# Half of the residual's transposes taken over by transposing transfers, at six of eight stage inputs

## The chip, the cores and the metric

The kernel runs on one core of a Trainium2 chip. A core has a matrix engine (TensorE, "PE" in the profile; its weight loads are "PEld"), three engines for elementwise work (VectorE "DVE", ScalarE "ACT", GpSimd "POOL"), and SyncE ("SP"), which here only issues DMA transfers. Matmuls write into PSUM banks; everything else lives in SBUF. The metric is the device time of one execution in microseconds (us); less is better.

## The reference

A decoder trunk of two layers on a stream `h` of 256 rows by 1024 columns, float32. Each layer has a half-step SwiGLU ffn, a token mixer (layer 0: a gated linear recurrence; layer 1: attention with a forget gate) and another ffn, each between two RMS norms. Layer 1's keys, values and gates come from the stream as it is after layer 0.

```python
for layer in range(DEPTH):
    if layer == N_A_LAYERS:
        k, v, c = shared_kv(h, kv_norm_g, w_kv, w_fgate, b_fgate)
    f = swiglu(rms_norm(h, ffn1_pre_g[layer]), ...)          # (silu(x @ w_gate) * (x @ w_up)) @ w_down
    h = h + 0.5 * rms_norm(f, ffn1_post_g[layer])
    hn = rms_norm(h, mix_pre_g[layer])
    m = recurrent_block(hn, ...) if layer < N_A_LAYERS else forgetting_attention(hn, ...)
    h = h + rms_norm(m, mix_post_g[layer])
    f = swiglu(rms_norm(h, ffn2_pre_g[layer]), ...)
    h = h + 0.5 * rms_norm(f, ffn2_post_g[layer])
```

What matters for the change is the step between two sub-layers: `h` is updated, and the next matmuls need `h`, scaled by a gain per column, with its columns on the partitions, that is, transposed.

## The kernel before

The 256 rows are two row tiles, t = 0 and t = 1, of 128 rows each. `h[t]` is 128 partitions by 1024 columns. A matmul contracts over partitions, so the input of a projection is kept as eight **k tiles**, each 128 columns of `h` transposed to 128 by 128.

All products are float32 made of two parts: each weight is split into `whi` (a rounded copy, ScalarE, L173) and `wlo` (the rest, VectorE, L177); each input into `xhi` (ScalarE, L235) and `xlo` (VectorE, L240). Three matmuls stand for one: hi by hi, hi by lo, lo by hi (L183 to L185, L428 to L432).

The weights come in units of up to 128 by 1024, loaded by SyncE into one of five raw buffers (`raw`) and split into one of nine pairs. One unit used for one row tile is a slot of six matmuls of 512 columns, some 1.36 us. `run()` interleaves the two row tiles: tile 0 is some slots ahead of tile 1, and each unit is used by both. `defer(n, fn)` calls `fn` n + 1 slots later, so the place at which something is issued hangs on the count of slots. TensorE's order is that of the code. On the other engines a scheduler chooses the order, with two means to steer it: `tc.high_priority()`, and `tc.keep_in_program_order`, which pins an instruction among the others so pinned.

**A stage's end** is `enter(t, dests, ...)` (L271). ScalarE sums squares of the accumulators (`junk`, L205), GpSimd makes `nv` and `rstd` (L198, L200), VectorE multiplies the accumulators by the gain (`t`, from PSUM, L284), and then updates `h` in two halves of 512 columns (L297). Some slots later (`defer(wait, inputs)`) comes `inputs()`: eight PE transposes (L226, `to_tp`, four for each half of the columns, into a PSUM bank each); per destination VectorE multiplies a bank by the next norm's gains (`xg`, L234), ScalarE makes `xhi` of it, VectorE `xlo`; and `stat(t)` starts the next norm's sums (ScalarE L205, GpSimd L198 and L200). There is one destination, save after layer 0, where there are two: layer 1's ffn (`xhi`, `xlo`) and the shared keys and values (`zhi`, `zlo`).

**The transposing transfer** is in the kernel already, for the ffn's products and for keys and queries: `planes` (GpSimd copies float32 into two planes of 16-bit halves; L210, L527), `swap` (SyncE issues a DMA that transposes 16-bit blocks of 128 by 128; L214, L535; pinned in SyncE's order), `join` (GpSimd copies the turned halves back into float32; L218, L540).

The eight stage inputs that `inputs()` serves, by the time of their transposes in the profile:

| | stage that ends | tile | transposes at, us | destinations |
|---|---|---|---|---|
| unchanged | mixer, layer 0 | 0 | 296.64 | 1 |
| place 1 | mixer, layer 0 | 1 | 304.52 | 1 |
| place 2 | second ffn, layer 0 | 0 | 475.42 | 2 |
| place 3 | second ffn, layer 0 | 1 | 485.84 | 2 |
| place 4 | first ffn, layer 1 | 0 | 703.31 | 1 |
| unchanged | first ffn, layer 1 | 1 | 713.72 | 1 |
| place 5 | mixer, layer 1 | 0 | 771.37 | 1 |
| place 6 | mixer, layer 1 | 1 | 783.14 | 1 |

Of the kernel before, what the change touches and what calls it, by code (L numbers as in the profile page):

```python
# [9 lines left out]
F32 = mybir.dt.float32  # L10
# [33 lines left out]
def trunk_kernel(ctx: ExitStack, tc: tile.TileContext, A: dict, out: bass.AP):  # L44
# [13 lines left out]
    def nm(s):  # L58
        uid[0] += 1
        return f"{s}_{uid[0]}"  # L60
# [168 lines left out]
    def x_upper(tp, dest, n):  # L229

        gi, xh, xl = dest
        xg = hpool.tile([P, 4, P], F32, tag="t1", name=nm("xg"), bufs=2)
        g = gT[:, gi + 4 * n:gi + 4 * n + 4].unsqueeze(2).to_broadcast([P, 4, P])
        nc.vector.tensor_tensor(xg, tp.rearrange("p (a b) -> p a b", a=4), g, ALU.mult)  # L234
        nc.scalar.activation(xh[:, 4 * n:4 * n + 4, :], xg, AF.Copy)  # L235
        return xg

    def x_lower(xg, dest, n):
        gi, xh, xl = dest
        nc.vector.tensor_tensor(xl[:, 4 * n:4 * n + 4, :], xg, xh[:, 4 * n:4 * n + 4, :].bitcast(F32), ALU.subtract)  # L240

    def to_x(tps, dest):

        with tc.high_priority():
            xg = [x_upper(tps[n], dest, n) for n in range(2)]
            for n in range(2):
                x_lower(xg[n], dest, n)

    def to_x_tiles(tps, dest):

# [15 lines left out]
    def stat(t):  # L266
        ss = new_ss()
        square_sum(h[t], ss[:, 0:1])
        rs[t] = rstd_of(ss, 1)

    def enter(t, dests, pf, gb, half, last=False, normed=False, wait=3):  # L271

        f = 1.0 / 16 if half else 1.0 / 32
        ss = new_ss()
        t1 = []
        urgent = tc.high_priority()
        urgent.__enter__()
        for n in range(2):
            square_sum(pf[n], ss[:, n:n + 1], f)
        for n in range(2):  # L280
            if n == 1 and last:
                r = rstd_of(ss, 2, f, nc.vector)
            t1.append(hpool.tile([P, 512], F32, tag="t1", name=nm("t1"), bufs=2))
            nc.vector.tensor_tensor(t1[n], pf[n], gb[:, n * 512:(n + 1) * 512], ALU.mult)  # L284
        if not last:
            r = rstd_of(ss, 2, f)

        sp, aq = nc.sync, nc.scalar
        pieces = [(n * 512, 512, None) for n in range(2)]
        if last:  # L290
            pieces = ([(0, 1024, sp)] if t == 0 else
                      [(0, 256, sp), (256, 256, aq), (512, 256, sp), (768, 256, aq)])
        for c, m, q in pieces:
            hn = h[t][:, c:c + m]
            for a in range(c, c + m, 512):
                n = min(m, 512)
                nc.vector.scalar_tensor_tensor(h[t][:, a:a + n], t1[a // 512][:, a % 512:a % 512 + n], r[:, 0:1],  # L297
                                               h[t][:, a:a + n], ALU.mult, ALU.add)
            if last:
                q.dma_start(out[0, t * P:(t + 1) * P, c:c + m], hn)  # L300
        urgent.__exit__(None, None, None)
        if last:
            return

        def inputs():
            tps = [to_tp(h[t], n) for n in range(2)]
            for dest in dests:
                to_x(tps, dest)
            stat(t)

        def norm():
            with tc.high_priority():
                normed_x()

        def normed_x():
            ss = new_ss()
            for n in range(2):
                square_sum(h[t][:, n * 512:(n + 1) * 512], ss[:, n:n + 1])
            rs[t] = rstd_of(ss, 2)
            hn = []  # L320
            for n in range(2):
                hn.append(hpool.tile([P, 512], F32, tag="t1", name=nm("hn"), bufs=2))
                nc.vector.tensor_scalar(hn[n], h[t][:, n * 512:(n + 1) * 512], rs[t][:, 0:1], None, ALU.mult)

            def go():
                tps = []
                for n in range(2):
                    tp = gtbank()
                    for j in range(4):
                        nc.tensor.transpose(tp[:, j * P:(j + 1) * P], hn[n][:, j * P:(j + 1) * P], ident)  # L330
                    tps.append(tp)
                to_x_tiles(tps, dests[0])
            defer(6, go)

        if normed:
            norm()
            settled[0] = True
        else:
            defer(wait, inputs)
# [152 lines left out]
    def ahead(i, fn):  # L492
# [5 lines left out]
            return prep()  # L498
        items[i] = (both, work)

    def ffn_items(pool_of, wg, wu, wd, post_g, next_dests, last=False, normed=False):
        hid = {}
        sil = {}
        box = {}

        def hid_tiles(t):
            if t not in hid:
                hid[t] = (pool_of().tile([P, 22, P], F32R, tag=f"hhi{t}", name=nm("hhi"), bufs=1),
                          pool_of().tile([P, 22, P], F32R, tag=f"hlo{t}", name=nm("hlo"), bufs=1))
            return hid[t]  # L510

        def post_gate(c0, nn):
            def f(t, ps):
                s = pool_of().tile([P, 512], F32, tag="sil", name=nm("sil"), bufs=2)
                nc.scalar.activation(s[:, :nn], ps, AF.Silu, scale=rs[t][:, 0:1])  # L515
                sil[t] = s
            return f

        def post_up(c0, nn):
            def f(t, ps):  # L520
                hh, hl = hid_tiles(t)
                s = sil[t][:, :nn]
                pr = pool_of().tile([P, 512], F32, tag="prod", name=nm("prod"), bufs=2)
                nc.vector.scalar_tensor_tensor(pr[:, :nn], ps, rs[t][:, 0:1], s, ALU.mult, ALU.mult)  # L524
                halves = hpool.tile([P, 512], F32, tag="t1", name=nm("pl"), bufs=2).bitcast(U16)[:, :2 * nn]
                turned = pr.bitcast(U16)[:, :2 * nn].rearrange("p (a b) -> p a b", b=P)
                nc.gpsimd.tensor_copy(halves.rearrange("p (h f) -> p h f", h=2),  # L527
                                      pr[:, :nn].bitcast(U16).rearrange("p (f h) -> p h f", h=2))
                defer(2, lambda: hidden_T(halves, turned, hh, hl))

            def hidden_T(halves, turned, hh, hl):

                m, k0 = nn // P, c0 // P
                keep = tc.keep_in_program_order
                keep(nc.sync.dma_start(turned, halves, transpose=True))  # L535
                hv = hh[:, k0:k0 + m, :].rearrange("p a b -> p (a b)")
                lv = hl[:, k0:k0 + m, :].rearrange("p a b -> p (a b)")

                def join():
                    nc.gpsimd.tensor_copy(halves.rearrange("p (f h) -> p h f", h=2),  # L540
                                          turned.rearrange("p (h a) b -> p h (a b)", h=2))

                def parts():
                    x = halves.bitcast(F32)
                    keep(nc.scalar.activation(hv, x, AF.Copy))  # L545
                    keep(nc.vector.tensor_tensor(lv, x, hv.bitcast(F32), ALU.subtract))  # L546
                defer(3, join)
                defer(7, parts)
            return f

        i0 = len(items)
        for i in range(5):
            proj_items(wg, i * 512, 512, main_x, post_gate(i * 512, 512))
            proj_items(wu, i * 512, 512, main_x, post_up(i * 512, 512))

        last_up = post_up(2560, 256)

        def post_both(t, pg, pu):
            post_gate(2560, 256)(t, pg)
            last_up(t, pu)  # L560

        pair_items(wg, wu, 2560, 256, main_x, post_both)

        def load_gb():
            box["gb"] = gain_bcast(post_g)

        ahead(i0 + 24, load_gb)

        def post_down(t, accs):
            enter(t, next_dests(t), accs, box["gb"], True, last, normed)  # L570

        row_items(wd, [P] * 22, lambda t, k: (hid[t][0][:, k, :], hid[t][1][:, k, :]), post_down, 4 if last else 2)
        return i0

# [644 lines left out]
    def post_q(n):  # L1219
        return lambda t, ps: heads_T(ps, t, n, HD ** -0.5, att["q"][t])  # L1220

    for n in range(2):
        proj_items(A["attn_w_q"][0], n * 512, 512, main_x, post_q(n))
    n_q[0] = len(items)
    row_items(A["attn_w_o"][0], [P] * 8, lambda t, k: (att["oh"][t][:, k, :], att["ol"][t][:, k, :]),
              lambda t, accs: enter(t, [main_dest(GI[("ffn2", 1)], t)], accs, gbox["mix1"], False, wait=4),
              rows0=1, late=True)
    ahead(n_q[0] + 2, load_gb("mix1", A["mix_post_g"][1]))
    n_att = len(items)
# [240 lines left out]
```

## Time and profile before

| | |
|---|---|
| median of three runs | 966.05 us (965.71 to 967.69) |
| the profiled execution | 965.92 us, its span 964.2 us |
| granted TensorE clock | 0.999 |
| TensorE busy | 955.9 us, 99% of the span |
| VectorE, ScalarE, GpSimd busy | 640.7, 527.6, 218.2 us |
| PE transposes of `h` (L226) | 64, in eight groups of 0.87 to 0.88 us |

A row of the timeline reads: start and length in us, engine, line, operation, output <- inputs, their shapes, how many alike follow one another (x2), and in brackets the idle time before it and what released it. Rows of the chain in order of time have a start, a length and what it was. Lines are those of the kernel before; in the kernel after they are higher by 14 from L270 on and by up to 35 further down.

### The profile page before, as it was taken

The numbers are of one execution on the slowest core, as the hardware profiler recorded it, in microseconds if no ns is written. First come the engines' busy times: TensorE is split into PE (matmuls) and PEld (weight loads), VectorE is DVE, ScalarE is ACT, GpSimd is POOL, SyncE is SP. The second block draws the span as 40 slices with busy tenths as digits, with TensorE's granted clock in tenths as the row PEclk, the third lists the DMA queues.
The fourth block names the chain that finished last, engine by engine and source line by source line (L and its number), as shares of the span: only waits on it lengthen the run. The fifth ranks groups of instructions, "written<-read, shape, count | busy, mean of one in ns | idle before, by whom it ended". The sixth has DMA issues, their size and how long they took to land.

```text
span 964.2 us, 12866 instructions
## 1 busy us (share of the span) xinstructions
PE 955.9 (99%) x4575; PEld 791.3 (82%) x4575; DVE 640.7 (66%) x845; ACT 527.6 (55%) x750; POOL 218.2 (23%) x221
## 2 busy tenths in 40 slices
PE   9999999999999999999999999999999999999997
PEld 6888888898878888888898888888887788888886
DVE  6658674678997666664686566665488876666642
ACT  7546453568886555443565455444366855444431
POOL 2712330130001323230003522234022012232200
PEclk9999999999999999999999999999999999999999
DMA  8787995475346787775558979878773468777731
GB/s 286 226 258 225 256 284 197 142 228 163 119 123 219 209 236 211 205 242 196 135 182 278 253 219 258 230 216 265 226 256 97 133 199 236 207 222 233 223 109 44
DMA packets 148934, 198.79 MB, mean 206 GB/s; under 512 B 67166, under 2 KB 85958, under 8 KB 148742
## 3 DMA queue, kind: packets, MB, share of 16 engines
q1 hardware_dynamic: 146182, 191.06, 65.6%
q0 software_dynamic: 2080, 6.38, 2.1%
q8 instruction: 36, 0.59, 0.2%
q10 hardware_dynamic: 608, 0.53, 0.2%
q14 instruction: 28, 0.23, 0.1%
HBM read 182.19 MB, written 3.16 MB: 192 GB/s over the span
## 4 chain that ended last, share of the span: by engine, by line
PE 95%; DVE 2%; ACT 1%; issue 1%; POOL 0%; DMA 0%; POOLq 0%; DVEq 0%; ACTq 0%
PE mm L428 16%; PE mm L429 16%; PE mm L432 16%; PE mm L183 13%; PE mm L185 13%; PE mm L184 13%; PE gt L795 2%; PE mm L1305 1%; PE mm L190 1%; PE mm L191 1%; PE mm L192 1%; PE gt L226 1%; ACT pe L1181 1%; DVE wlo L177 0%; PE tr L127 0%
## 5 line engine op out<-in xcount | busy, mean ns | idle before, releaser
L177 DVE TENSOR_TENSOR wlo<-raw,whi 128x1024 fp32r<-128x1024 f32 (+5 forms) x329 | 418.0, 1276 | 230.7 <-ACT whi L173 228.3
L173 ACT ACTIVATE whi<-raw 128x1024 fp32r<-128x1024 f32 (+5 forms) x329 | 341.9, 1045 | 308.6 <-PE mm L432 119.2
L428 PE MATMUL mm<-whi,xhi 128*128 128x512 f32 x656 | 256.6, 391 | 0.0
L429 PE MATMUL mm<-wlo,xhi 128*128 128x512 f32 x656 | 255.5, 389 | 0.0
L432 PE MATMUL mm<-whi,xlo 128*128 128x512 f32 x656 | 202.1, 389 | 0.0
L428 PEld LDWEIGHTS mm<-whi,xhi 128*128 128x128 f32 x656 | 123.2, 188 | 25.9 <-issue 0.7
L432 PEld LDWEIGHTS mm<-whi,xlo 128*128 128x128 f32 x656 | 123.1, 188 | 25.8 <-DVE xlo L240 0.2
L429 PEld LDWEIGHTS mm<-wlo,xhi 128*128 128x128 f32 x656 | 123.2, 188 | 25.4 <-DVE wlo L177 0.3
L183 PE MATMUL mm<-whi,hhi 128*128 128x512 f32 x352 | 137.2, 390 | 0.0
L185 PE MATMUL mm<-whi,hlo 128*128 128x512 f32 x352 | 137.0, 389 | 0.0
L184 PE MATMUL mm<-wlo,hhi 128*128 128x512 f32 x352 | 136.9, 389 | 0.0
L540 POOL COPY pl<-prod 128x1024 uint16<-128x1024 uint16 (+1 forms) x48 | 69.9, 1456 | 174.4 <-DMA prod<-pl 174.4
L527 POOL COPY pl<-prod 128x1024 uint16<-128x1024 uint16 (+1 forms) x48 | 66.3, 1382 | 151.9 <-DVE prod L524 86.8
L183 PEld LDWEIGHTS mm<-whi,hhi 128*128 128x128 f32 x352 | 66.1, 188 | 13.7
L185 PEld LDWEIGHTS mm<-whi,hlo 128*128 128x128 f32 x352 | 66.1, 188 | 13.7
L184 PEld LDWEIGHTS mm<-wlo,hhi 128*128 128x128 f32 x352 | 66.1, 188 | 13.6
L198 POOL TENSOR_SCALAR nv<-ss 128x1 f32<-128x1 f32 x22 | 9.6, 437 | 268.7 <-ACT junk L205 268.7
L524 DVE SCALAR_TENSOR_TENSOR prod<-mm,rstd,sil 128x512 f32<-128x512 f32 (+1 forms) x48 | 33.8, 703 | 29.5 <-PE mm L432 25.9
L515 ACT ACTIVATE sil<-mm,rstd 128x512 f32<-128x512 f32 (+1 forms) x48 | 31.0, 649 | 32.9 <-PE mm L432 25.0
L546 DVE TENSOR_TENSOR hlo<-pl,hhi 128x512 fp32r<-128x512 f32 (+1 forms) x48 | 41.2, 858 | 3.7 <-ACT hhi L545 3.7
L183 PE MATMUL mm<-whi,xhi 128*128 128x512 f32 (+1 forms) x112 | 42.8, 382 | 0.0
L185 PE MATMUL mm<-whi,xlo 128*128 128x512 f32 (+1 forms) x112 | 42.5, 379 | 0.0
(223 smaller groups left out, 1054.6 us busy)
## 6 DMA issues: line engine op xcount, KB each, us to landing
raw<-in_ffn_w_down_dram SPq DMA_DIRECT2D x88, 512.0 KB
raw<-in_ffn_w_up_dram SPq DMA_DIRECT2D x80, 512.0 KB
raw<-in_ffn_w_gate_dram SPq DMA_DIRECT2D x78, 512.0 KB
raw<-in_rg_w_in_dram SPq DMA_DIRECT2D x10, 504.0 KB
raw<-in_rg_w_out_dram SPq DMA_DIRECT2D x10, 504.0 KB
raw<-in_ffn_w_gate_dram SPq DMA_DIRECT2D x19, 256.0 KB
raw<-in_ffn_w_up_dram SPq DMA_DIRECT2D x16, 256.0 KB
raw<-in_rg_w_in_dram SPq DMA_DIRECT2D x8, 512.0 KB
```

The lines of the kernel that those rows point to most:

```text
L173: up = nc.scalar.activation(hi[:parts, c:c + m], rawv[:, c:c + m], AF.Copy)
L177: nc.vector.tensor_tensor(lo[:parts, c:c + m], rawv[:, c:c + m], hi[:parts, c:c + m].bitcast(F32), ALU.subtract)
L183: nc.tensor.matmul(ps, xh, wh, start=first, stop=False)
L184: nc.tensor.matmul(ps, xh, wl, start=False, stop=False)
L185: nc.tensor.matmul(ps, xl, wh, start=False, stop=last)
L428: nc.tensor.matmul(ps, get_x(t, k)[0], u.hi[:, c], start=k == 0, stop=False)
L429: nc.tensor.matmul(ps, get_x(t, k)[0], u.lo[:, c], start=False, stop=False)
L432: nc.tensor.matmul(ps, get_x(t, k)[1], u.hi[:, c], start=False, stop=k == nk - 1)
L524: nc.vector.scalar_tensor_tensor(pr[:, :nn], ps, rs[t][:, 0:1], s, ALU.mult, ALU.mult)
L527: nc.gpsimd.tensor_copy(halves.rearrange("p (h f) -> p h f", h=2), pr[:, :nn].bitcast(U16).rearrange("p (f h) -> p h f", h=2))
L540: nc.gpsimd.tensor_copy(halves.rearrange("p (f h) -> p h f", h=2), turned.rearrange("p (h a) b -> p h (a b)", h=2))
L546: keep(nc.vector.tensor_tensor(lv, x, hv.bitcast(F32), ALU.subtract))
```

## The change

At places 1 to 6 the columns 512 to 1023 of `h` (k tiles 4 to 7) no longer go through PE transposes. Right after `h` is updated, GpSimd copies them into planes. `inputs()` makes four transposes in place of eight, and after `stat(t)` SyncE issues the transposing transfer; one slot later GpSimd is given the joining copy, and two (tile 0) or four (tile 1) slots later the joined tile is scaled on VectorE per destination (from SBUF; `turned_to_x`), copied into `xhi` on ScalarE and subtracted into `xlo` on VectorE. The scale and the copy are pinned in their engines' order. The buffers: for tile 0 old buffers of the ffn's products, or of the queries; for tile 1 the buffers named "t1" and "junk". Two stage inputs stay as they were.

```diff
     def to_x(tps, dest):
         with tc.high_priority():
-            xg = [x_upper(tps[n], dest, n) for n in range(2)]
-            for n in range(2):
-                x_lower(xg[n], dest, n)
+            xg = [x_upper(tp, dest, n) for n, tp in enumerate(tps)]
+            for n, v in enumerate(xg):
+                x_lower(v, dest, n)
+
+    def turned_to_x(v, dests, more):
+        with tc.high_priority():
+            xs = []
+            for i, (gi, xh, xl) in enumerate(dests):
+                xg = v if i == len(dests) - 1 else more()
+                g = gT[:, gi + 4:gi + 8].unsqueeze(2).to_broadcast([P, 4, P])
+                xs.append(xg.rearrange("p (a b) -> p a b", a=4))
+                tc.keep_in_program_order(
+                    nc.vector.tensor_tensor(xs[i], v.rearrange("p (a b) -> p a b", a=4), g, ALU.mult))
+                tc.keep_in_program_order(nc.scalar.activation(xh[:, 4:, :], xs[i], AF.Copy))
+            for xg, dest in zip(xs, dests):
+                x_lower(xg, dest, 1)
...
-    def enter(t, dests, pf, gb, half, last=False, normed=False, wait=3):
+    def enter(t, dests, pf, gb, half, last=False, normed=False, wait=3, spare=None):
...
+        by_transfer = not normed and (spare or t == 1) and not (half and len(dests) == 1 and t == 1)
+        if by_transfer:
+            a = spare() if t == 0 else hpool.tile([P, 512], F32, tag="t1", name=nm("hp"), bufs=2)
+            with tc.high_priority():
+                planes(a.bitcast(U16), h[t][:, 512:])
+
         def inputs():
-            tps = [to_tp(h[t], n) for n in range(2)]
+            tps = [to_tp(h[t], n) for n in range(1 if by_transfer else 2)]
             for dest in dests:
                 to_x(tps, dest)
             stat(t)
+            if by_transfer:
+                b = spare() if t == 0 else spool.tile([P, 512], F32, tag="junk", name=nm("ht"), bufs=1)
+                with tc.high_priority():
+                    swap(b.bitcast(U16), a.bitcast(U16))
+                defer(0, lambda: join(a.bitcast(U16).rearrange("p (f h) -> p h f", h=2), b.bitcast(U16)))
+                defer(1 + 2 * t, lambda: turned_to_x(a, dests, spare))
...
+    def old_products():
+        return pools["f"].tile([P, 512], F32, tag="prod", name=nm("hp"), bufs=2)
...
-            enter(t, next_dests(t), accs, box["gb"], True, last, normed)
+            enter(t, next_dests(t), accs, box["gb"], True, last, normed, spare=old_products)
...
+    q_parts = [1, 0]
+
+    def old_q():
+        return att["q"][0].rearrange("p a b -> p (a b)").rearrange("p (s f) -> p s f", s=2)[:, q_parts.pop(), :]
...
-              lambda t, accs: enter(t, [main_dest(GI[("ffn2", 1)], t)], accs, gbox["mix1"], False, wait=4),
+              lambda t, accs: enter(t, [main_dest(GI[("ffn2", 1)], t)], accs, gbox["mix1"], False, wait=4,
+                                    spare=old_q),
```

**VectorE at place 2**, from the update of `h0` (tile 0) to that of `h1` (tile 1), before; a name's number only tells buffers apart, `gt` is a bank of transposes:

```order
L297 SCALAR_TENSOR_TENSOR h_74<-t_807_4254,rstd_4258,h_74 128x512
L177 TENSOR_TENSOR wlo_4271<-raw_4268,whi_4270 128x1024
L177 TENSOR_TENSOR wlo_4283<-raw_4280,whi_4282 128x1024
L234 TENSOR_TENSOR xg_4302<-gt_4292,gT 128x512
L234 TENSOR_TENSOR xg_4305<-gt_4297,gT 128x512
L177 TENSOR_TENSOR wlo_4329<-raw_4325,whi_4328 128x720
L240 TENSOR_TENSOR xlo<-xg_4302,xhi 128x4x128
L240 TENSOR_TENSOR xlo<-xg_4305,xhi 128x4x128
L234 TENSOR_TENSOR xg_4310<-gt_4292,gT 128x512
L234 TENSOR_TENSOR xg_4313<-gt_4297,gT 128x512
L177 TENSOR_TENSOR wlo_4342<-raw_4338,whi_4341 128x720
L240 TENSOR_TENSOR zlo_4246<-xg_4310,zhi_4245 128x4x128
```

(Then a second zlo, the two `t` and the two halves of `h1`.) The same stretch after, from the first xg on; `hp` is the joined tile, and L258 its scale:

```order
L234 TENSOR_TENSOR xg_4298<-gt_4293,gT 128x512
L234 TENSOR_TENSOR xg_4302<-gt_4293,gT 128x512
L177 TENSOR_TENSOR wlo_4319<-raw_4315,whi_4318 128x720
L240 TENSOR_TENSOR xlo<-xg_4298,xhi 128x4x128
L240 TENSOR_TENSOR zlo_4245<-xg_4302,zhi_4244 128x4x128
L177 TENSOR_TENSOR wlo_4333<-raw_4329,whi_4332 128x720
L258 TENSOR_TENSOR hp_4342<-hp_4261,gT 128x512
L298 TENSOR_TENSOR t_841_4380<-mm_3946,gb_3331 128x512
L258 TENSOR_TENSOR hp_4261<-hp_4261,gT 128x512
L240 TENSOR_TENSOR xlo<-hp_4342,xhi 128x4x128
L298 TENSOR_TENSOR t_842_4382<-mm_3947,gb_3331 128x512
L240 TENSOR_TENSOR zlo_4245<-hp_4261,zhi_4244 128x4x128
```

Two of four xg are gone, and two scales stand later, the first after the last wlo and the second between the two `t`; `h1` follows behind this row in both.

**VectorE at place 4**, from the two wlo behind `h0` to `h1`'s `t`, before:

```order
L177 TENSOR_TENSOR wlo_1211_6228<-raw_1209_6225,whi_1210_6227 128x1024
L177 TENSOR_TENSOR wlo_1214_6240<-raw_1212_6237,whi_1213_6239 128x1024
L234 TENSOR_TENSOR xg_1217_6259<-gt_1215_6249,gT_89 128x512
L234 TENSOR_TENSOR xg_1218_6262<-gt_1216_6254,gT_89 128x512
L177 TENSOR_TENSOR wlo_1225_6277<-raw_1223_6274,whi_1224_6276 128x1024
L240 TENSOR_TENSOR xlo_91<-xg_1217_6259,xhi_90 128x4x128
L240 TENSOR_TENSOR xlo_91<-xg_1218_6262,xhi_90 128x4x128
L177 TENSOR_TENSOR wlo_1228_6289<-raw_1226_6286,whi_1227_6288 128x1024
L177 TENSOR_TENSOR wlo_1231_6301<-raw_1229_6298,whi_1230_6300 128x1024
L284 TENSOR_TENSOR t1_1238_6327<-mm_1153_5890,gb_1024_5266 128x512
```

and after, from the xg on:

```order
L234 TENSOR_TENSOR xg_1217_6253<-gt_1216_6248,gT_89 128x512
L177 TENSOR_TENSOR wlo_1225_6269<-raw_1223_6266,whi_1224_6268 128x1024
L240 TENSOR_TENSOR xlo_91<-xg_1217_6253,xhi_90 128x4x128
L177 TENSOR_TENSOR wlo_1228_6282<-raw_1226_6279,whi_1227_6281 128x1024
L258 TENSOR_TENSOR hp_1209_6216<-hp_1209_6216,gT_89 128x512
L177 TENSOR_TENSOR wlo_1231_6297<-raw_1229_6294,whi_1230_6296 128x1024
L298 TENSOR_TENSOR t1_1238_6323<-mm_1153_5887,gb_1024_5263 128x512
L240 TENSOR_TENSOR xlo_91<-hp_1209_6216,xhi_90 128x4x128
L298 TENSOR_TENSOR t1_1239_6325<-mm_1154_5888,gb_1024_5263 128x512
L311 SCALAR_TENSOR_TENSOR h1_75<-t1_1238_6323,rstd_1241_6329,h1_75 128x512
```

Here the scale stands ahead of the last wlo, and its xlo between the two `t`.

**GpSimd at place 2**, from tile 0's `rstd` on, after; before, the three rows with `hp` or of its joining are not there, and the rest stands in the same order:

```order
L200 TENSOR_TENSOR rstd_809_4257<-nv_808_4255,mhalf_85 128x1
L212 COPY hp_810_4261<-h0_74 128x1024
L198 TENSOR_SCALAR nv_822_4309<-ss_820_4306 128x1
L200 TENSOR_TENSOR rstd_823_4311<-nv_822_4309,mhalf_85 128x1
L220 COPY hp_810_4261<-hp_824_4313 128x2x512
L198 TENSOR_SCALAR nv_843_4384<-ss_838_4375 128x1
L200 TENSOR_TENSOR rstd_844_4386<-nv_843_4384,mhalf_85 128x1
L212 COPY hp_845_4390<-h1_75 128x1024
```

The planes copy (L212) has come in behind tile 0's `rstd`, and the joining copy (L220) ahead of the `nv` and `rstd` from which tile 1's `h` is updated.

## The prediction

> **What bounds the kernel now.** I read the page's first part and its chain first, then the chain in order of time around the transposes, then VectorE's and TensorE's rows at each place.
>
> ```profile
> PE 955.9 (99%) x4575; PEld 791.3 (82%) x4575; DVE 640.7 (66%) x845; ACT 527.6 (55%) x750; POOL 218.2 (23%) x221
> PE 95%; DVE 2%; ACT 1%; issue 1%; POOL 0%; DMA 0%; POOLq 0%; DVEq 0%; ACTq 0%
> ```
>
> TensorE is busy for 955.9 of 964.2 us and carries 95% of the chain. So a microsecond taken from TensorE is a microsecond gained, as long as its inputs are there; and a microsecond for which it waits is lost whole, because nothing behind it has slack to give back. The other engines have room on average, but the average doesn't tell about the stage ends, where the change acts.
>
> **What is removed.** At each of the six places four of eight PE transposes go. The chain in order of time (start, length, what) has these groups, place 1 to place 6:
>
> ```profile
> 304.52 0.87 PE gt L226 x8
> 475.42 0.87 PE gt L226 x8
> 485.84 0.87 PE gt L226 x8
> 703.31 0.87 PE gt L226 x8
> 771.37 0.88 PE gt L226 x8
> 783.14 0.87 PE gt L226 x8
> ```
>
> Eight cost 0.87, so four cost 0.435, and six places give 6 x 0.435 = 2.61 us. All of it lies on the chain. That is the most that the change can bring: 965.92 - 2.61 = 963.3 against the profiled execution's own 965.92 us (0.13 below the median of the runs, which I neglect). VectorE keeps its count: where it multiplied a transposed bank (xg, read from PSUM), it now multiplies the joined tile (the scale, read from SBUF), once per destination.
>
> **What is added, alone.** Per place a copy into planes and a joining copy on GpSimd, and one transposing transfer on SyncE. The kernel has all three already, on the ffn's products. Rows of GpSimd, of SyncE's queue, of the chain and of the waits (total us, count, longest):
>
> ```profile
> 49.99 1.04 POOL L527 COPY pl<-prod 128x1024 uint16<-128x1024 uint16 x1 [3.13 <-DVE prod L524]
> 51.05 1.24 SPq L535 DMA_TRANSPOSE prod<-pl  x1
> 56.78 1.34 POOL L540 COPY pl<-prod 128x1024 uint16<-128x1024 uint16 x1 [5.76 <-DMA prod<-pl]
> 732.70 3.06 DMA htok<-pl
> POOL pl L540 <- DMA prod<-pl: 174.4, 46, 10.1
> ```
>
> Planes take 1.04, SyncE's issue 1.24, the joining copy 1.34. From issue to joined copy it is 3.1 in a quiet queue (the row at 732.70), 5.7 where other transfers stand in the way (51.05 to 56.78), 3.8 on the mean over 46 waits (174.4 / 46), 10.1 at the worst. At places 2 and 4 the transfer stands ahead of the next weight load in SyncE's order, and the loads before it were issued long ago or wait behind it, so I take 3.1 to 3.5 there. The weight loads behind it are held for the 1.24 us of the issue and for GpSimd's planes; five raw buffers stand between a load and its use, so I cost that at nothing. If that cover went, it would cost up to 1.24 a place.
>
> **What the copies do to VectorE.** A planes copy and a joining copy, each beside VectorE's work, then hlo alone, and a joining copy with a VectorE row that reads PSUM:
>
> ```profile
> 361.88 1.22 DVE L177 TENSOR_TENSOR wlo<-raw,whi 128x1024 fp32r<-128x1024 f32 x1
> 363.01 1.53 DVE L546 TENSOR_TENSOR hlo<-pl,hhi 128x512 fp32r<-128x512 f32 x1
> 362.09 1.90 POOL L527 COPY pl<-prod 128x1024 uint16<-128x1024 uint16 x1 [5.84 <-ACT hhi L545]
> ...
> 91.38 1.79 DVE L546 TENSOR_TENSOR hlo<-pl,hhi 128x512 fp32r<-128x512 f32 x1
> 90.44 2.25 POOL L540 COPY pl<-prod 128x1024 uint16<-128x1024 uint16 x1 [6.65 <-DMA prod<-pl]
> ...
> 64.80 0.68 DVE L546 TENSOR_TENSOR hlo<-pl,hhi 128x512 fp32r<-128x512 f32 x1
> 101.34 2.32 POOL L540 COPY pl<-prod 128x1024 uint16<-128x1024 uint16 x1 [3.21 <-DMA prod<-pl]
> 102.37 0.74 DVE L524 SCALAR_TENSOR_TENSOR prod<-mm,rstd,sil 128x512 f32<-128x512 f32 x1
> ```
>
> The planes copy at 362.09 begins during a wlo and takes 1.90 where it takes 1.04 alone: it stood for 0.86 until that wlo ended at 363.10. Then hlo took 1.53 where it takes 0.68 alone, 0.85 more. With the joining copy at 90.44 it is 2.25 for 1.34, and hlo 1.79, which is 1.11 more. So the two engines exclude each other here, and VectorE pays 0.85 per planes copy and 1.11 per joining copy. The row at 102.37 reads PSUM, lies inside the joining copy at 101.34, and takes 0.74; its group of 48 has a mean of 0.70 (x48, 703 ns on the page), so it is not delayed. Bounds of one pair: 0 where both copies fall beside PSUM readers or gaps, 0.85 + 1.11 = 1.96 where VectorE runs on SBUF operands without a gap. Whether this matters depends on VectorE's slack at the place.
>
> The Trainium skill, page "SBUF — State Buffer", section "SBUF: two separate sides", has a rule for this: VectorE with two SBUF inputs and a GpSimd operation that reads SBUF take an exclusive lock for a whole instruction, and the loser fully blocks. By that rule a pair would cost the whole of both copies, 1.04 + 1.34 = 2.38, and the sum below would come to 967.6 in place of 966.8; the rows above agree on who blocks whom, and show 0.85 and 1.11.
>
> **Place 2 (end of layer 0's second ffn, tile 0).** VectorE, and TensorE's rows as tile 1's transposes begin (place 3):
>
> ```profile
> 473.20 1.41 DVE L297 SCALAR_TENSOR_TENSOR h<-t,rstd,h 128x512 f32<-128x512 f32 x2 [0.36 <-POOL rstd L200]
> 474.53 2.35 DVE L177 TENSOR_TENSOR wlo<-raw,whi 128x1024 fp32r<-128x1024 f32 x2
> 476.80 1.28 DVE L234 TENSOR_TENSOR xg<-gt,gT 128x512 f32<-128x512 f32 x2
> ...
> 481.22 0.90 DVE L177 TENSOR_TENSOR wlo<-raw,whi 128x720 fp32r<-128x720 f32 x1
> 482.03 1.29 DVE L240 TENSOR_TENSOR zlo<-xg,zhi 128x512 fp32r<-128x512 f32 x2
> 483.24 1.28 DVE L284 TENSOR_TENSOR t<-mm,gb 128x512 f32<-128x512 f32 x2
> 484.44 1.40 DVE L297 SCALAR_TENSOR_TENSOR h<-t,rstd,h 128x512 f32<-128x512 f32 x2
> 485.22 0.62 PE L432 MATMUL mm<-whi,xlo 128*128 128x512 f32 x2
> 485.68 1.03 PE L226 MATMUL gt<-ident,h 128*128 128x128 f32 x8
> ```
>
> From 473.20 to 485.84 no row of VectorE shows idle time after the first. Tile 1's first half of h ends at 484.44 + 0.70 = 485.14, and the transposes that read it start at 485.68. TensorE would now arrive 0.435 earlier, at 485.24, and meets a slack of 0.10. In the new order VectorE still does its work of the same count ahead of that h, two scales in place of two xg. The planes copy falls on the two wlo (the first ends near 475.7, so planes run to 476.8); the transfer starts at about 476.8 and, at 3.1 to 3.5, the joining copy starts at 479.9 to 480.3, where VectorE has xlo, zlo and wlo, all on SBUF. So both are paid: h at 485.14 + 0.85 + 1.11 = 487.10, and TensorE waits 487.10 - 485.24 = 1.86 us. Small waits of TensorE for tile 0's late x (scale, then xhi, then xlo) lie inside this, since they come before the same wait. Low end 0 (copies beside PSUM readers), high end 2.3 (whole copies).
>
> **Place 3 (the same end, tile 1).** The row of TensorE that first needs k tiles 4 and 5 of tile 1:
>
> ```profile
> 495.53 0.39 PE L428 MATMUL mm<-whi,xhi 128*128 128x512 f32 x1
> ```
>
> Now it would be 495.53 - 0.87 + 1.86 = 496.5. The way to it: h whole at 485.84 + 1.96 = 487.8, planes 1.04 to 1.90, transfer 3.1 to 3.8 behind two loads, joining copy 1.34 to 2.25, scale 0.68, xhi about 0.63 (xg and xhi are of one size): 494.6 to 497.1. That is between 1.9 early and 0.6 late; I take 0.3.
>
> **Place 4 (end of layer 1's first ffn, tile 0).**
>
> ```profile
> 702.44 2.35 DVE L177 TENSOR_TENSOR wlo<-raw,whi 128x1024 fp32r<-128x1024 f32 x2
> 708.25 2.36 DVE L177 TENSOR_TENSOR wlo<-raw,whi 128x1024 fp32r<-128x1024 f32 x2
> 711.73 1.42 DVE L297 SCALAR_TENSOR_TENSOR h<-t,rstd,h 128x512 f32<-128x512 f32 x2
> 713.56 1.04 PE L226 MATMUL gt<-ident,h 128*128 128x128 f32 x8
> ```
>
> Tile 1 is not changed here, but it waits for VectorE: its h half is there at 711.73 + 0.71 = 712.44, TensorE arrives at 713.56 - 0.435 = 713.12, slack 0.68. Planes fall on the wlo pair at 702.44, the joining copy near 708 on wlo and xlo. 712.44 + 1.96 = 714.40, a wait of 1.28 us. Ends: 0 and 1.7. Here the pinned scale is close as well. Its turn comes at about 709.3 (wlo, wlo, xg, wlo, xlo, wlo from 702.44, and 0.85), the transfer starts at 704.7, so with the joining copy's 1.34 it has 709.3 - 704.7 - 1.34 = 3.3 us to land.
>
> **Places 1, 5 and 6.**
>
> ```profile
> 303.10 1.42 DVE L297 SCALAR_TENSOR_TENSOR h<-t,rstd,h 128x512 f32<-128x512 f32 x2 [0.31 <-POOL rstd L200]
> 316.13 0.39 PE L428 MATMUL mm<-whi,xhi 128*128 128x512 f32 x1
> 779.82 1.42 DVE L297 SCALAR_TENSOR_TENSOR h<-t,rstd,h 128x512 f32<-128x512 f32 x2 [0.24 <-POOL rstd L200]
> ```
>
> At place 1 h is whole at 304.52, k tiles 4 and 5 are needed at 316.13 - 0.44 = 315.7, which leaves 11.2; the way takes 1.04 to 1.90, a wait for SyncE of about 1, 3.1 to 3.8, 1.34 to 2.25, 0.68 and 0.63, together 7.8 to 10.3: hidden. Place 6 has the same spacing (783.14, some 10 us to k tiles 4 and 5), hidden. At place 5 what could be late is tile 1's h: half of it is there at 780.53, over 2.4 before the transposes at 783.14 - 0.435 = 782.7, and VectorE was waiting for rstd just before it (0.24), so the copies delay it by less than that. Hidden too. For these three I cost the additions at nothing; cover gone, one place costs at most its pair, 1.96.
>
> **The sum.** -2.61 + 1.86 + 0.3 + 1.28 = +0.83, so 965.92 + 0.83 = 966.8 us. About 0.2% (1.93 us) is what a measurement of this kernel can tell from no change, so this is within it.
>
> **The rivals.**
> A, the copies cost VectorE nothing that TensorE sees. For it: PSUM readers are not delayed, and xg and t read PSUM. Against: at both places the copies fall on wlo and xlo. All stalls gone gives 963.3; it needs stalls of under 0.7 in all to count as faster.
> B, slower: the transfer of place 4 lands late, and the scale, fixed in VectorE's order ahead of t and h, holds both. For it: 3.8 is the mean, 5.7 was seen, and only 3.3 is free. Against: no load is in front. With 5.7 it costs 5.7 - 3.3 = 2.4 more: 969.2. It turns the result to slower from a landing of 3.3 + (1.93 - 0.83) = 4.4 us on.
> C, the change is hidden in part: only one of places 2 and 4 stalls. 965.92 - 2.61 + 0.3 + 1.28 or + 1.86 gives 964.9 or 965.5, within 0.2%; I count it to the forecast.
>
> **Chances.** Forecast with C 0.50, A 0.19, B 0.31. The range goes from A's 963.4 to B's 969.4. The likeliest one's own range is 964.9 to 967.8.
>
> **What would show it.** Groups of x4 transposes at six places and 40 transposes in all; VectorE without idle from 474 to 487, with a wlo or xlo 0.8 to 1.1 longer beside each new copy; TensorE idle, released by VectorE's h, 1.9 at about 485 and 1.3 at about 713; nothing at places 1, 5, 6. Wrong would be: those waits under 0.3 (A), an idle VectorE ahead of a scale, released by GpSimd's joining copy (B), or TensorE waiting for weights behind the held loads, which I cost at nothing.

## The result and the profile after

The changed kernel takes 968.49 us (median of 12 runs, 967.98 to 970.32) where the kernel before takes 965.71 in the same comparison: 1.0024 of its time, 95% interval 1.0016 to 1.0032. So it is slower by about a quarter of a percent. The time lies inside the stated range and 1.7 us above the predicted 966.8. It lies 0.7 us above 967.8, the upper end that the likeliest case has for itself, and the 2.78 us lost are more than the 1.93 that the prediction counts as no change.

The page of the profile after (its execution took 968.89 us), first part and chain:

```profile
span 967.2 us, 12833 instructions
PE 955.2 (99%) x4551; PEld 787.8 (81%) x4551; DVE 647.1 (67%) x845; ACT 527.9 (55%) x750; POOL 243.4 (25%) x233
PE 91%; DVE 3%; issue 2%; ACT 2%; DMA 1%; POOL 1%; POOLq 0%; ACTq 0%; DVEq 0%
```

TensorE's share of the chain has fallen from 95% to 91%. Where its time went is seen by matching its matmuls one to one between the two traces, transposes left out, and following how far each lies behind its partner (us, after minus before):

| from the row above to | shift | change |
|---|---|---|
| 271 us | 0.59 | +0.59 |
| behind place 1 | 0.16 | -0.43 |
| behind place 2's own transposes | -0.27 | -0.44 |
| behind place 2's wait, and place 3 | 1.63 | +1.90 (-0.44 and 2.34 of waits) |
| behind place 4's own transposes | 1.23 | -0.40 |
| attention's first matmuls | 3.24 | +2.01 (waits) |
| behind places 5 and 6 | 2.40 | -0.84 |
| the end of the span | 2.97 | +0.57 |

The gains are as forecast: each place frees 0.40 to 0.44 us, 2.6 in all. The waits are 2.34 and 2.01. The six places together cost 2.40 - 0.59 = 1.81 us. Two parts lie outside: 0.59 at the first weight load, and 0.57 behind the last matmul.

**Place 2.** VectorE, GpSimd and TensorE after, from tile 0's h to tile 1's transposes:

```profile
474.70 3.19 DVE L177 TENSOR_TENSOR wlo<-raw,whi 128x1024 fp32r<-128x1024 f32 x2
...
480.44 1.79 DVE L240 TENSOR_TENSOR zlo<-xg,zhi 128x512 fp32r<-128x512 f32 x1
482.15 0.89 DVE L177 TENSOR_TENSOR wlo<-raw,whi 128x720 fp32r<-128x720 f32 x1
482.97 0.68 DVE L258 TENSOR_TENSOR hp<-hp,gT 128x512 f32<-128x512 f32 x1
...
486.57 1.41 DVE L311 SCALAR_TENSOR_TENSOR h<-t,rstd,h 128x512 f32<-128x512 f32 x2
474.85 1.97 POOL L212 COPY hp<-h 128x1024 uint16<-128x1024 uint16 x1 [1.51 <-DVE h L311]
479.94 1.80 POOL L220 COPY hp<-hp 128x1024 uint16<-128x1024 uint16 x1 [1.31 <-DMA hp<-hp]
487.37 0.66 PE L226 MATMUL gt<-ident,h 128*128 128x128 f32 x4 [1.13 <-DVE h L311]
```

The two wlo take 3.19 where they took 2.35 (+0.84, the planes copy at 474.85), and zlo takes 1.79 where one takes 0.68 (+1.11, the joining copy at 479.94). The transfer landed 3.1 after its issue at 476.85, ahead of the scale's turn, so no row shows VectorE waiting for it. TensorE waits for h.

**Place 4.** The chain in order of time (start, length, what) up to tile 1's transposes:

```profile
707.55 4.11 DMA raw<-in_attn_w_q_dram
...
712.01 0.49 ACT whi L173
712.50 0.48 issue
712.98 0.61 ACT xhi L259
713.59 0.58 ACT junk L205 x2
714.18 0.10 issue
714.27 0.68 POOL nv L198
...
715.03 0.57 POOL rstd L200
715.60 0.03 issue
715.63 0.76 DVE h L311
716.39 0.04 issue
716.43 0.67 PE gt L226 x4
717.11 0.08 issue
717.19 0.63 PE gt L226 x4
```

and the rows of SyncE's queue, ScalarE and VectorE that belong to it:

```profile
706.22 1.24 SPq L216 DMA_TRANSPOSE hp<-hp  x1
707.55 0.53 SPq L161 DMA_DIRECT2D raw<-in_attn_w_q_dram  x1
712.01 1.06 ACT L173 ACTIVATE whi<-raw 128x1024 fp32r<-128x1024 f32 x1 [1.01 <-DMA raw<-in_attn_w_q_dram]
715.63 1.41 DVE L311 SCALAR_TENSOR_TENSOR h<-t,rstd,h 128x512 f32<-128x512 f32 x2 [0.24 <-POOL rstd L200]
```

VectorE loses its two copies here too (its wlo rows: 3.19 for two at 704.08, and 2.32 for one at 709.53). But the chain that ends last is another: the weight load that stands behind the transfer in SyncE's queue, issued at 707.55. Before, it was issued at 703.69, right behind the first of the two wlo (it ended at 703.66), which with the shift of 1.2 to 1.6 is about 705. ScalarE's whi waits 1.01 for it, then come the pinned xhi, tile 1's second square sum, nv and rstd, and h waits 0.24 for rstd. Then the transposes of the second half of h wait once more: four at 716.43, four at 717.19, where eight had run through in 0.87.

### The profile page after: what moved, and what is told of

The parts are those of the page before. It is cut to its first block, busy times and chain, and to the rows that moved or that the text cites. A ratio compares the mean times of both kernels' runs of the same rounds, so it can differ in the third digit from the quotient of the medians.

```text
span 967.2 us, 12833 instructions
## 1 busy us (share of the span) xinstructions
PE 955.2 (99%) x4551; PEld 787.8 (81%) x4551; DVE 647.1 (67%) x845; ACT 527.9 (55%) x750; POOL 243.4 (25%) x233
## 4 chain that ended last, share of the span: by engine, by line
PE 91%; DVE 3%; issue 2%; ACT 2%; DMA 1%; POOL 1%; POOLq 0%; ACTq 0%; DVEq 0%
PE mm L454 16%; PE mm L458 16%; PE mm L455 16%; PE mm L183 12%; PE mm L185 12%; PE mm L184 12%; PE gt L824 2%; PE mm L1340 1%; PE mm L190 1%; PE mm L191 1%; PE mm L192 1%; DVE wlo L177 1%; ACT pe L1210 1%; DVE h L311 0%; PE gt L226 0%
## 5 line engine op out<-in xcount | busy, mean ns | idle before, releaser
L177 DVE TENSOR_TENSOR wlo<-raw,whi 128x1024 fp32r<-128x1024 f32 (+5 forms) x329 | 423.1, 1292 | 217.0 <-ACT whi L173 215.5
L569 POOL COPY pl<-prod 128x1024 uint16<-128x1024 uint16 (+1 forms) x48 | 69.4, 1446 | 171.7 <-DMA prod<-pl 171.7
L556 POOL COPY pl<-prod 128x1024 uint16<-128x1024 uint16 (+1 forms) x48 | 69.0, 1437 | 139.9 <-DVE prod L553 76.2
L198 POOL TENSOR_SCALAR nv<-ss 128x1 f32<-128x1 f32 x22 | 12.2, 555 | 241.0 <-ACT junk L205 241.0
```

The source lines that it names most:

```text
L177: nc.vector.tensor_tensor(lo[:parts, c:c + m], rawv[:, c:c + m], hi[:parts, c:c + m].bitcast(F32), ALU.subtract)
```

## The experiments

Each kernel was timed beside the kernel before, in 4 to 12 runs. "Shift" is that of the last matmul against the kernel before, less that at 250 to 270 us; "end" is from the end of the last matmul to the end of the span (6.10 before). Both are of the one profiled execution.

| kernel | median, us | before, us | ratio (95%) | shift | end |
|---|---|---|---|---|---|
| the change | 968.49 | 965.71 | 1.0024 (1.0016 to 1.0032) | +1.8 | 6.67 |
| places 1, 5, 6 | 964.79 | 965.86 | 0.9988 (0.9979 to 0.9997) | -1.3 | 6.43 |
| places 2, 3, 4 | 968.90 | 965.86 | 1.0032 (1.0019 to 1.0044) | +2.7 | 6.44 |
| places 1, 3, 5, 6 | 964.54 | 965.86 | 0.9985 (0.9976 to 0.9994) | -1.6 | 6.36 |
| one more copy at 2, 4 | 969.68 | 965.86 | 1.0038 (1.0026 to 1.0051) | +3.3 | 6.65 |
| copies on ScalarE at 2, 4 | 966.21 | 965.78 | 1.0006 (0.9997 to 1.0015) | -0.2 | 6.67 |
| copies alone at 2, 4 | 966.58 | 965.78 | 1.0008 (0.9999 to 1.0017) | +0.9 | 6.09 |
| a seventh place | 972.43 | 965.78 | 1.0073 (1.0059 to 1.0087) | +5.4 | 6.73 |
| place 4's transfer from ScalarE | 972.44 | 965.85 | 1.0067 (1.0050 to 1.0083) | +6.7 | 6.24 |

**Which places lose.** Three kernels are the change with another set of places:

```diff
+        place = (2 + t if len(dests) == 2 else 4) if half else (5 + t if spare else 1)
+        by_transfer = by_transfer and place in (1, 5, 6)       # or (2, 3, 4), or (1, 3, 5, 6)
```

> Transfers at places 1, 5 and 6 alone (the mixers' ends). Theory (what is lost is lost at the ffn ends, where VectorE runs without a gap): three times 0.43 us gained, no wait of TensorE for h: 965.7 - 1.3 = 964.4 us, up to 965.6 if the 0.6 us at the start and the 0.57 us at the end that the changed kernel's profile shows outside the places come along. Rival (a transfer costs about the same at each place, 2.8 / 6 = 0.46 us net): 967.1 us.

> Transfers at places 2, 3 and 4 alone (the ffns' ends). Theory: 3 times 0.43 gained, waits of 2.0, 0.3 and 2.0 us as in the changed kernel: 965.7 + 3.1 = 968.8 us, 969.9 us with the offsets at start and end. Rival (the same cost at each place): 967.1 us.

> The changed kernel without places 2 and 4, so with 1, 3, 5 and 6. Theory: the two waits of 2.0 us are gone, four times 0.43 us are gained and place 3's wait of 0.3 stays or goes: 964.0 to 964.3 us, 965.4 us with the offsets. Rival (the copies are not the cause, the waits come from elsewhere): 967.5 us or more.

964.79, 968.90 and 964.54 us: the theory's numbers each time, and the even price per place is out (967.1 was wanted twice). A transfer is a gain at the mixers' ends and for tile 1 at the end of layer 0's second ffn, and a loss for tile 0 at the ffns' ends. TensorE at places 3 and 4 in the last of these kernels:

```profile
484.38 0.62 PE L460 MATMUL mm<-whi,xlo 128*128 128x512 f32 x2
484.84 0.60 PE L226 MATMUL gt<-ident,h 128*128 128x128 f32 x4
485.19 0.48 PE L456 MATMUL mm<-whi,xhi 128*128 128x512 f32 x1
...
712.38 1.03 PE L226 MATMUL gt<-ident,h 128*128 128x128 f32 x8
```

No row has a bracket: TensorE waits for nothing. Without tile 0's transfers place 3 loses next to nothing either (0.05 by the matched matmuls, where the change lost 0.33).

**Do GpSimd's copies hold VectorE?** One more copy behind the joining copy, which nothing needs:

```diff
+                    join(a.bitcast(U16).rearrange("p (f h) -> p h f", h=2), b.bitcast(U16))
+                    if place in (2, 4):
+                        planes(b.bitcast(U16), a)
```

> The changed kernel with one more planes copy on GpSimd behind the joining copy at places 2 and 4; nothing waits for its output, and VectorE's order stays. Theory (GpSimd's copies hold VectorE, and VectorE's h holds TensorE): 0.85 to 1.1 us more at each, so 968.5 + 1.7 to 2.2 = 970.2 to 970.7 us. Rival (TensorE waits for late transfers or for ScalarE): no change, 968.5 us.

VectorE and GpSimd in it, at place 2 and place 4:

```profile
481.62 1.74 DVE L177 TENSOR_TENSOR wlo<-raw,whi 128x720 fp32r<-128x720 f32 x1
481.27 1.33 POOL L212 COPY hp<-hp 128x1024 uint16<-128x1024 uint16 x1
...
713.13 0.69 DVE L258 TENSOR_TENSOR hp<-hp,gT 128x512 f32<-128x512 f32 x1 [0.93 <-POOL hp L212]
```

At place 2 a wlo takes 1.74 in place of 0.89: 0.85 for the one copy, and the wait of TensorE grows by as much (0.84). At place 4 the copy is itself held by a wlo, and VectorE's scale, which writes into the tile that the copy reads, waits 0.93 for it: a dependence between two tiles, and not what was meant to be tested. So of the two places one shows what was meant. The median rose by 1.2, less than the 1.7 to 2.2 expected (at place 4, h no longer waits for rstd in this kernel, which hides some of it), and the rival's "no change" is out.

The copies taken off GpSimd:

```diff
-    def planes(dst, src):
+    def planes(dst, src, act=False):
...
+        if act:
+            nc.scalar.activation(d, s, AF.Copy)
+        else:
+            nc.gpsimd.tensor_copy(d, s)
```

> The changed kernel with the planes copy and the joining copy of places 2 and 4 on ScalarE in place of GpSimd; the transfer, the pinned scale and the rest stay. Theory (VectorE is held by GpSimd's copies): wlo and xlo there take what they take alone, VectorE's h is 1.9 us earlier at both places, and of the two waits of 2.0 us at most 0.5 each is left, save what ScalarE's two more copies delay (its square sums, and with them rstd): 964.5 to 966.5 us. Rival (the transfer's landing or the scale fixed in VectorE's order makes the wait): 968 us or more.

```profile
474.32 2.36 DVE L177 TENSOR_TENSOR wlo<-raw,whi 128x1024 fp32r<-128x1024 f32 x2
...
480.20 1.36 ACT L224 ACTIVATE hp<-hp 128x1024 uint16<-128x1024 uint16 x1 [0.84 <-DMA hp<-hp]
481.60 0.69 DVE L264 TENSOR_TENSOR hp<-hp,gT 128x512 f32<-128x512 f32 x1 [0.89 <-ACT hp L224]
486.01 0.66 PE L232 MATMUL gt<-ident,h 128*128 128x128 f32 x4 [0.42 <-DVE h L317]
...
714.47 1.04 PE L232 MATMUL gt<-ident,h 128*128 128x128 f32 x8
```

966.21 us. The wlo are back at 2.36, and no row of VectorE is longer for a copy. At place 4 tile 1's transposes wait for h no more (714.47, no bracket); at place 2 0.42 of that wait is left. So the wait for h goes with the copies' engine. In its place comes another: the joined tile is late. At place 2 ScalarE's joining copy waits 0.84 for the landing (4.2 us after the issue here, with a load issued 0.47 ahead of the transfer), and VectorE's scale waits 0.89 for that copy; at place 4 the late xhi holds TensorE. By the matched matmuls places 2 and 3 have 1.5 us of waits in place of 2.34, and place 4 has 0.91 in place of 2.01: about half is left, where at most 0.5 each was expected, and it eats the gain.

The copies without the transfer, in the kernel before:

```diff
+        copies = by_transfer and place in (2, 4)
+        by_transfer = False
...
+            if copies:
+                b = spare()
+                defer(1, lambda: join(b.bitcast(U16).rearrange("p (f h) -> p h f", h=2), a.bitcast(U16)))
```

> The kernel before with all its transposes, and at places 2 and 4 a planes copy at once followed by a joining copy into a spare tile that nothing reads; no transfer, no scale. Theory (only VectorE rows that read SBUF alone are held): the planes copy holds a wlo by 0.85 us, the second copy falls beside the two xg, which read PSUM, and holds nearly nothing; TensorE has 0.54 and 1.1 us of slack there, so it loses 0.3 to 0.6 us at place 2 and nothing at place 4: 966.1 to 966.4 us, and the end behind the last matmul stays at 6.1 us. Rival (each GpSimd copy holds VectorE, whatever stands beside it): 1.42 + 0.84 us lost, 968.1 us.

```profile
474.20 3.20 DVE L177 TENSOR_TENSOR wlo<-raw,whi 128x1024 fp32r<-128x1024 f32 x2
477.32 1.28 DVE L234 TENSOR_TENSOR xg<-gt,gT 128x512 f32<-128x512 f32 x2
476.38 2.25 POOL L220 COPY hp<-hp 128x1024 uint16<-128x1024 uint16 x1
485.85 1.29 PE L226 MATMUL gt<-ident,h 128*128 128x128 f32 x8 [0.34 <-DVE h L311]
```

966.58 us, where 966.1 to 966.4 was expected and 968.1 by the rival. The first copy costs VectorE 0.85 (3.20 for 2.35). The second runs beside the two xg, which read PSUM, and they take 1.28 as ever. So it is not the copy that costs, but what stands beside it. By the matched matmuls TensorE loses 0.75 and 0.17, more than the slack of 0.54 and 1.1 leaves. In part that is because the expectation, like the prediction's sum, goes by the first half of h, and the last four transposes wait for the second half as well (0.2 and 0.1 us of the two losses).

**What the unchanged place would have done.**

```diff
+        place = (2 + t if len(dests) == 2 else 4 + 3 * t) if half else (5 + t if spare else 1)
+        by_transfer = not normed and (spare or t == 1) and place in (1, 3, 5, 6, 7)
```

> The kernel of places 1, 3, 5 and 6, and in addition a transfer at the place that the change leaves out (first ffn of layer 1, tile 1). Theory (a tile-1 transfer has slots enough before its k tiles are needed): 0.43 us more gained, less 0.1 at the end, 964.2 us. Rival (attention starts there, its small steps on VectorE and GpSimd stand behind the copies): 965 us or more.

```profile
714.34 0.63 POOL L1039 DMA_DIRECT2D bias<-bias1d  x1
714.42 1.24 SPq L216 DMA_TRANSPOSE ht<-hp  x1
726.02 1.31 POOL L220 COPY hp<-ht 128x1024 uint16<-128x1024 uint16 x1 [10.46 <-DMA ht<-hp]
```

and its waits (total us, count, longest), TensorE's longest:

```profile
PE tr L1058 <- DVE htok L1045: 5.6, 1, 5.6
```

972.43 us, far past the rival's 965. A large transfer (attention's bias, 128 x 4096) is issued from GpSimd at 714.34, the transposing one right behind it at 714.42, and its joining copy begins 11.6 us after that, in place of 3.1. The kernel before has a pair like it, a transposing transfer at 578.81 behind one of 1 MB (`bias1d`) issued 0.08 earlier; its joining copy begins 11.2 later:

```profile
589.99 2.20 POOL L540 COPY pl<-prod 128x1024 uint16<-128x1024 uint16 x1 [10.13 <-DMA prod<-pl]
```

That the large transfer is the cause is read from these two pairs; no run takes it away. The scale is fixed in VectorE's order and VectorE stands idle for 9.90 before it, so htok, some rows behind it, is late and TensorE waits 5.6. This is the mechanism of the prediction's rival B, at a place that the change doesn't touch. When TensorE goes on, its granted clock is 0.50 for some 3 us (730 to 733), and about 1 us more is lost.

**The weight load behind the transfer.** Place 4's transfer issued from ScalarE's queue, so that the load isn't behind it:

```diff
-                    swap(b.bitcast(U16), a.bitcast(U16))
+                    swap(b.bitcast(U16), a.bitcast(U16), nc.scalar if place == 4 else nc.sync)
```

> The changed kernel with place 4's transposing transfer issued from ScalarE's queue in place of SyncE's, so that no weight load stands behind it (the scheduler also puts tile 1's second square sum ahead of place 4's xhi there). Theory (at place 4 some 0.3 us of the wait of 2.0 come from the held load: ScalarE's whi waits for it 1.0 us, and with it the square sums, nv, rstd and h): that wait of ScalarE for the load is gone and VectorE's h is not released by rstd; but ScalarE now waits for GpSimd's planes and issues for 1.2 us, so its next whi is 1.9 us later and VectorE loses about as much on that wlo as it gains: 968.0 to 968.9 us. Rival (the held load has nothing to do with it): VectorE's h is still released by rstd with ScalarE waiting for the same load.

```profile
704.62 0.37 SPq L161 DMA_DIRECT2D raw<-in_attn_w_q_dram  x1
705.52 1.33 ACTq L216 DMA_TRANSPOSE hp<-hp  x1
706.60 4.76 SPq L164 DMA_DIRECT2D raw<-in_attn_w_o_dram  x3
710.90 1.05 ACT L173 ACTIVATE whi<-raw 128x1024 fp32r<-128x1024 f32 x1
713.77 1.32 POOL L220 COPY hp<-hp 128x1024 uint16<-128x1024 uint16 x1 [6.46 <-DMA hp<-hp]
715.12 0.72 DVE L258 TENSOR_TENSOR hp<-hp,gT 128x512 f32<-128x512 f32 x1 [4.11 <-POOL hp L220]
```

ScalarE's whi has no wait for its load any more: that part of the theory holds. That h isn't released by rstd says little, since VectorE comes to h (718.70) 3 us later than in the change. And the time was missed by 4 us. The joining copy begins 8.2 us after the transfer's issue (705.52 to 713.77), and VectorE stands idle for 4.11 at the pinned scale. The load at 704.62 is now ahead of the transfer, and those from 706.60 on are no longer held behind it. A load ahead doesn't explain it alone: at places 1 and 6 of the change one stands 0.85 ahead in the same queue, and the joining copy begins 5.2 after the issue. Whether the other loads or ScalarE's queue make the rest, no run separates.

The wait is not the whole loss either. TensorE's first matmul behind it, and the stretches that follow (from and to, length, busy time of PE, PEld, VectorE, ScalarE and GpSimd, granted clock, DMA share, GB/s):

```profile
716.55 0.79 PE L455 MATMUL mm<-whi,xhi 128*128 128x512 f32 x1 [3.66 <-ACT xhi L259]
716.00:719.00 3.00, 2.45 (x6) 1.69 (x6) 3.00 (x5) 2.93 (x4) 0.84 (x2) 0.50 0.56 128
```

The granted clock is 0.50 up to about 722.7, and the matmuls start 0.43 apart where 0.23 is usual. By the matched matmuls 3.8 us are lost in the wait and 3.1 more in that stretch, most of it by these slower steps. Behind the change's own waits (0.86 to 1.13 of idle time) the clock stays at 1.00.

The kernel of places 2, 3 and 4 says more of the held load. It has the same transfer with the same load behind it, but ScalarE's whi waits less for that load, and h isn't released by rstd:

```profile
711.15 1.06 ACT L173 ACTIVATE whi<-raw 128x1024 fp32r<-128x1024 f32 x1 [0.53 <-DMA raw<-in_attn_w_q_dram]
714.92 1.40 DVE L311 SCALAR_TENSOR_TENSOR h<-t,rstd,h 128x512 f32<-128x512 f32 x2
```

TensorE loses 1.66 at place 4 there, and 2.01 in the change. So some 0.35 hang on the chain through ScalarE and rstd. In that chain the pinned xhi (0.61) stands beside the wait for the load (1.01), and neither was taken out by itself.

**Better than both.** The kernel with places 1, 3, 5 and 6 takes 964.54 us, 0.9985 of the kernel before (0.9976 to 0.9994). It is the change without tile 0 at the ffns' ends.

## Why the prediction was right or wrong

- **What is removed** (0.435 per place, 2.61 in all): right. The matched matmuls show 0.40 to 0.44 at each place.
- **What the copies do to VectorE** (0.85 and 1.11): right to 0.01 at place 2, 0.84 and 1.11; and the exception for PSUM readers is shown by the copies alone. By the Trainium skill's rule (page "SBUF — State Buffer", section "SBUF: two separate sides") a whole copy would be lost each time; the trace agrees on who blocks whom, and a planes copy of 1.04 cost 0.84 to 0.85 wherever it was measured (places 2 and 4, and two further kernels).
- **Place 2** (1.86): nearly right, 2.01: small waits for tile 0's late xhi and xlo 0.67, then 1.34 for h. That they lie inside the sum is as forecast.
- **Place 3** (0.3): 0.33. That it is a result of place 2's delay, and not of its own transfer, the kernel without places 2 and 4 shows. The closeness is partly luck: the prediction's own span went from 1.9 early to 0.6 late, and it gave no reason for 0.3.
- **Places 1, 5, 6** (nothing lost): right, by the kernel with these alone. The working for place 5 has two slips that change nothing: 782.7 less 780.53 is 2.2, not over 2.4, and a wait of 0.24 for rstd doesn't bound what the copies can delay.
- **Place 4** (1.28, its ends 0 and 1.7): mis-sized; 2.01, outside its own ends. VectorE's part came as summed: its second `t` ends at 715.38, which would put TensorE 1.3 late. The step that failed is "the weight loads behind it are held ... so I cost that at nothing". The five raw buffers were no cover there, since before, the load was issued the moment a buffer came free; after, it came some 2 us late, and through whi, the pinned xhi, the square sums and rstd it put h back by 0.24 of idle time, some 0.3 with the overlap of two VectorE rows that goes with it. Some 0.35 more came from the second half of h, for which the last four transposes wait, a wait that the sum left out. The kernel of places 2, 3 and 4 bears this out: without the wait for rstd 1.66 are lost, which is 1.3 and 0.35. How much of the 0.3 is the held load's and how much the pinned xhi's stays open.
- **The part outside the places** wasn't in the sum at all. The last matmul is followed by 6.09 to 6.10 us in the two kernels without transfers, and by 6.24 to 6.73 in those with three to six. In the changed kernel it is 6.67, so 0.57 more than before. It is not a price per transfer: three give 6.43 and 6.44, four 6.36. The trace shows a part of it. SyncE closes with eight waits in a fixed order, one for each of the semaphores that the transfers signal in turn, and a wait that finds its semaphore ready takes 0.06 to 0.09. Before, the last store of the result signals the last of the eight. With three, four and six transfers more it signals the third, the fourth and the sixth, so that five, four and two waits stand behind its own, which is 0.30, 0.24 and 0.16 us. The other 0.4 of the changed kernel lies around SyncE's last drains; the kernels with one more copy, with the copies on ScalarE and with a seventh place have it too, the one with place 4's transfer from ScalarE has not, and why is open. The 0.59 at the start is of this profiled execution; other kernels' starts lay between 0.4 earlier and 0.3 later, so I don't count it to the change.
- **The sum**: +0.83 forecast; +1.8 at the places and +0.57 at the end is +2.4, and the medians say +2.8. The remaining 0.4 is not explained. That 968.5 lies inside the range owes something to luck: the range reaches to 969.4 for the sake of B, and B didn't happen; the likeliest case's own range ended at 967.8.
- **The rivals.** A (hidden copies) is out for the change, but it is what the kernel without places 2 and 4 does. C is out: both places stalled. B (a late landing holds the pinned scale) didn't happen: the two transfers landed in about 3.1 us. Its mechanism is real, and two experiments met it, with joining copies that begin 8.2 and 11.6 us after the issue.

## What to carry to other kernels

Work moved off the bottleneck engine is not free because its new engine has room on average: the price is what stands beside it at that moment, so look at whether VectorE's rows there read SBUF or PSUM, and at how much slack the next row that TensorE waits for has. Here the same transfer gains 0.4 us where VectorE has gaps and loses 1.6 where it has 0.1 to 0.7 us of slack. And a transfer put ahead of loads in a queue delays those loads (here by 2 us), while one that has a load or a large transfer just ahead of it lands late (here after 4 to 12 us in place of 3): cost both, with the row that waits next.

## What the runs showed of the hardware that was not expected

- The joining copy begins 3.1 us after the issue of the transposing transfer at places 2 and 4, although three loads were issued behind it meanwhile. With a load 0.85 us ahead in the queue it is 5.2 at places 1 and 6 and 3.7 at place 3. From ScalarE's queue, with loads on SyncE's around it, it is 8.2, and 11.6 behind a 128 x 4096 transfer issued 0.08 us earlier.
- Where TensorE had stood idle for 3.7 us (place 4's transfer from ScalarE) and for 5.6 us (a seventh place), its granted clock was 0.50 afterwards, for some 6 and 3 us. After 1.1 us it was 1.00.
- The time from the last matmul to the end of the span differs with the number of transfers far ahead of it, and not steadily: 6.10 us with none added, 6.43 and 6.44 with three, 6.36 with four, 6.73 with five, 6.24 to 6.67 with six.
- ScalarE makes the same planes copy in 1.04 us and the joining copy in 1.36 (GpSimd 1.04 and 1.34 alone), and VectorE's rows beside them keep their length (two wlo 2.36, one of 128x720 0.90).
